# Reordering an eight-core decoder kernel: service order on ACT and DVE, one ones-matmul per norm, norms beside matmuls, gated first loads

## The chip, the cores and the metric

One Trainium2 chip, eight cores, the same program on each. The eight cores share the batch of 8 prompts and 32 samples: each takes one prompt of 2048 tokens (four tiles t0 to t3 of 512 tokens) and four samples of 8 tokens (one small tile TS of 32 tokens). The metric is the device time of the slowest core in microseconds (us), lower is better.

## The reference, cut to what matters

The function is one step of a two-layer decoder. Only its skeleton matters here: six RMS norms per tile, each of them in front of a large product.

```python
def rmsnorm(x, g):
    y = x * lax.rsqrt(jnp.mean(x * x, axis=-1, keepdims=True) + EPS)
    return y * g
# layer 0: x += 0.5*ffn(rms(x)); x += gla(rms(x));  x += 0.5*ffn(rms(x))
# shared:  k, v = proj(rms(x))                    (one norm statistic, two gains: this and the next FFN)
# layer 1: x += 0.5*ffn(rms(x)); x += attn(rms(x)); x += 0.5*ffn(rms(x))
def swiglu_ffn(x, w_in, w_out):           # 1024 -> 2*2688 -> 1024
    g, u = jnp.split(x @ w_in, 2, axis=-1)
    return (jax.nn.silu(g) * u) @ w_out
```

GLA is a gated linear attention, `attn` a dilated window attention over the shared keys and values.

## The kernel before

The kernel is a list scheduler that runs when the program is built. Every tile is a Python generator ("thread") that yields operations with their reads, writes and an estimated cost. The scheduler keeps a model time for each engine and each buffer and picks, again and again, among the operations that can start about earliest, the one of best rank to append next to its engine's list. Each engine is then given its list in exactly this order. So a choice made in the model is frozen into the order of instructions.

```python
class Sched:
    DMA_BW = 340e3                        # bytes per us, of the model
    # op(): tf = t0 + cost + (0.25 if eng == PE else 0.12)   <- when the model lets a dependent operation start

class Threads:
    TIE = 0.15
    def run(self):
        # ... cut: advance every thread to its next operation ...
        cands = [(S.start_of(...), th) for th in self.live if th[3] is not None]
        m = min(c[0] for c in cands) + self.TIE
        th = min((c for c in cands if c[0] <= m), key=lambda c: (rank of c, age of c))[1]
        # ... the operation of th is appended to its engine ...
```

Two of the four large tiles are in work at a time, each with its own ring of four weight units (`rings`, 8192 columns per partition each). The rank favours the first tile until it leads by 24 units, and favours the operations behind a matmul (`post`, `evac`) over the matmuls.

The norm computed the eight squares on ACT, summed them over partitions and over chunks by eight matmuls with a matrix of ones, and then applied the norm:

```python
    def norm_stats(T):
        # squares of 7 chunks must be in order before the first ones-matmul is
        yield mm(PS[b][:, 0:n], [(ones, T.h[:, m, :]) for m in range(7)], ...)
        yield mm(PS[b][:, 0:n], [(ones, T.h[:, 7, :])], ...)
        # Ln on ACT (with EPS), Exp(-0.5 x) on ACT
    def norm_apply(T, gcol, i):           # eight DVE operations h <- x * gain * rs
        for m in range(8): yield stt(T.h[:, m, :], T.x[:, m, :], ...)
```

Loads at the start: x of t0 and four weight units are issued first, x of t1 waits for weight unit 3, and the constants (`CF`) stand behind x in the issuing queue. In the trace of core 7 they are issued only at 25.8 us and land at 40.3 us.

The softmax here doesn't subtract the row's maximum and nothing guards it: scores larger than these inputs give would overflow.

Of the kernel before, what the change touches and what calls it, by code (L numbers as in the profile page):

```python
# [24 lines left out]
class Sched:  # L25



    DMA_BW = 340e3
    DMA_LAT = 2.2  # L30
# [16 lines left out]
    def _split(reads, writes):  # L47
# [4 lines left out]
        return reads, writes  # L52

    def start_of(self, eng, reads, writes):
        t = self.free[eng]
        reads, writes = self._split(reads, writes)
        for r in reads:
            k = self.lastw.get(r)
            if k is not None and k[3] > t:
                t = k[3]  # L60
        for w in writes:
            k = self.lastw.get(w)
            if k is not None and k[3] > t and not (k[2] == eng == PE):
                t = k[3]
            for k in self.readers.get(w, ()):
                if k[3] > t and not (k[2] == eng == PE):
                    t = k[3]
        return t
# [78 lines left out]
class Threads:  # L147
# [10 lines left out]
    def spawn(self, gen, rank, base=None):  # L158

        self.seq += 1  # L160
        self.live.append([rank, self.seq, gen, None, None, base or (lambda: 0)])

    def run(self):
        S = self.S
        while self.live:
# [34 lines left out]
            m = min(c[0] for c in cands) + self.TIE  # L200
            th = min((c for c in cands if c[0] <= m), key=lambda c: (c[1][0] + c[1][5](), c[1][1]))[1]
            _, eng, fn, reads, writes, cost, dma, nbytes = th[3]
# [16 lines left out]
def c_act(n):  # L219
    return 0.11 + n * 0.00083  # L220


def c_dve(n, rate=1):
    return 0.07 + n / (960.0 * rate)

# [72 lines left out]
def build():  # L298
# [116 lines left out]
    for t in range(4):  # L415
# [6 lines left out]
        def ffn_units(f):  # L422
            for j in range(NF):
                add_unit("fi%d" % f, j, wfi[f * NF + j], 2048)
            for m in range(8):
                add_unit("fo%d" % f, m, wfo[f * 8 + m], 2688)
        ffn_units(0)
        for gi, kind in enumerate(("v", "qk", "r", "o")):
            for i in range(4):
                add_unit(kind, i, wgl[gi * 4 + i], 2048)  # L430
            if t == 0 and kind == "qk":
                for s in range(4):
                    src = st_in[s * 4:(s + 1) * 4].rearrange("h p d -> p h d")
                    add_unit("S0", s, src, 2048, 1)
                    add_unit("S0b", s, src, 1024, 1)
        ffn_units(1)
# [16 lines left out]
    NWS = 8  # L453

    def weights(slot):
        ring = rings[slot]
        live = []
        off = 0
        if slot == 1:
            yield need(lambda: S.lastw.get(("x", "b1", 7)) is not None)  # L460
        for k, u in enumerate(order[slot]):
# [5 lines left out]
            yield need(lambda over=over: all(o.left == 0 for _, _, o in over))  # L467
            live = [x for x in live if x not in over] + [(lo, hi, u)]
            u.ap = ring[:, lo:hi]
            dst = u.ap  # L470
            if u.kind == "S0":
                dst = dst.bitcast(F32)
            if u.kind in ("S0", "S0b"):
                dst = dst.rearrange("p (h d) -> p h d", h=4)
            yield O(PL, (lambda e, u=u, dst=dst: e.dma_start(out=dst, in_=u.src)),  # L475
                    [("x", "b1", 1)] if u.uid == (1, "fi0", 0) else [], writes=[u.key] + [o.key for _, _, o in over], cost=1.0, dma="w%d_%d" % (slot, k % NWS), nbytes=u.n * 512)
            u.ready = True
# [126 lines left out]
    def load_x(T, prev):  # L604
        nq = 4 if T.n == 512 else 1
        if T.t == 1:
            yield need(lambda: units[(0, "fi0", 3)].ready)
        for q in range(nq):
            ms = range(q * 8 // nq, (q + 1) * 8 // nq)
            if prev is not None:  # L610
                yield need(lambda: all(("y", prev.nm, m) in done for m in ms))
            w = len(ms) * T.n
            src = xp[T.t] if T.n == 512 else xs
            yield O(SP, (lambda e, q=q, w=w, src=src, ms=ms: e.dma_start(
                out=T.x[:, ms[0]:ms[-1] + 1, :].rearrange("p m n -> p (m n)"), in_=src[:, q * w:(q + 1) * w])),
                [units[(0, "fi0", 3)].key] if T.t == 1 else [], writes=[xk(T, m) for m in ms], cost=0.1, dma="x%s_%d" % (T.b, q), nbytes=w * 512)
            for m in ms:
                yield square(T, m)
                done.add(("sq", T.nm, T.sqn, m))

    def square(T, m):
        return act(T.h[:, m, :], T.x[:, m, :], AF.Square, T.n, [xk(T, m)], [hk(T, m)], scale=1.0 / 32)

    def norm_stats(T):

        n = T.n
        sqn = T.sqn
        yield need(lambda: all(("sq", T.nm, sqn, m) in done for m in range(7)))
        (b,) = yield from get_banks(1)
        yield mm(PS[b][:, 0:n], [(ones, T.h[:, m, :]) for m in range(7)], [hk(T, m) for m in range(7)] + ["CB"], b, n, stop=False)  # L630
        yield need(lambda: ("sq", T.nm, sqn, 7) in done)
        yield mm(PS[b][:, 0:n], [(ones, T.h[:, 7, :])], [hk(T, 7), "CB"], b, n, start=False)
        (i,) = yield from T.pool.get("rs", 1, 1)
# [7 lines left out]

    def norm_apply(T, gcol, i):
        for m in range(8):
            yield stt(T.h[:, m, :], T.x[:, m, :], G[:, gcol + m:gcol + m + 1], T.pool.aps[i], ALU.mult, ALU.mult, T.n,
                      [xk(T, m), T.pool.key(i), "CF"], [hk(T, m)])

    def norm(T, gcol):
        i = yield from norm_stats(T)
        yield from norm_apply(T, gcol, i)
        T.pool.put("rs", i)  # L650

# [9 lines left out]
    def ffn(T, f, last):  # L661
# [14 lines left out]
        for j in range(NF):  # L676
# [8 lines left out]
            if j == 0 and n == 512:  # L685

                for kt in range(8):
                    for z, dst in ((0, g), (1, up)):
                        yield mm(dst, [(v[:, kt, z * 128:(z + 1) * 128], T.h[:, kt, :])], [hk(T, kt), u.key], bs[z], n, start=(kt == 0), stop=(kt == 7))
            else:  # L690
                yield mm(g, [(v[:, kt, 0:128], T.h[:, kt, :]) for kt in range(8)], hks(T) + [u.key], bs[0], n)
                yield mm(up, [(v[:, kt, 128:256], T.h[:, kt, :]) for kt in range(8)], hks(T) + [u.key], bs[-1], n)
# [21 lines left out]
    def tail(T, m, last):  # L714
# [7 lines left out]
        else:  # L722
            sqn = T.sqn
            yield square(T, m)
            done.add(("sq", T.nm, sqn, m))

# [6 lines left out]
    def gla(T):  # L733
# [4 lines left out]
        (b,) = yield from get_banks(1)  # L738
        yield mm(PS[b][0:16, :], [(WLR[:, kt, :], T.h[:, kt, :]) for kt in range(8)], h8 + ["WLR"], b, n)
        (gi,) = yield from pool.get("glr", 1, 1)  # L740
# [199 lines left out]
    def gla_s(T):  # L940
# [19 lines left out]
        (b,) = yield from get_banks(1)  # L960
        yield mm(PS[b][0:16, 0:n], [(WLR[:, kt, :], T.h[:, kt, :]) for kt in range(8)], h8 + ["WLR"], b, n)
        glr = R[0:16, 2432:2464]
# [62 lines left out]
        for s in range(4):  # L1025
            c8 = slice(s * 8, s * 8 + 8)
            us, ub = (yield from use(T, "S0", s)), (yield from use(T, "S0b", s))
            S0 = us.ap.bitcast(F32).rearrange("p (h w) -> p h w", h=4)
            S0b = ub.ap.rearrange("p (h w) -> p h w", h=4)
            (b,) = yield from get_banks(1)  # L1030
            po = PS[b][:, 0:64].rearrange("p (m n) -> p m n", m=8)
# [102 lines left out]
    def kv(T, tab):  # L1134
# [20 lines left out]
        u = yield from use(T, "kv", 0)  # L1155
        v = u.ap.rearrange("p (kt c) -> p kt c", kt=8)
        for kc in range(2):
            (b,) = yield from get_banks(1)
            yield mm(PS[b][:, 0:n], [(v[:, kt, kc * 128:(kc + 1) * 128], T.h[:, kt, :]) for kt in range(8)], h8 + [u.key], b, n)
            TH.spawn(kpost(kc, b), -4, T.rank)  # L1160
        u.left -= 1
# [45 lines left out]
    def qproj(T, tab):  # L1207
# [13 lines left out]
        for q in range(3):  # L1221
            u = yield from use(T, "wq", q)
            v = u.ap.rearrange("p (kt c) -> p kt c", kt=8)
            for z in range(2):
                (b,) = yield from get_banks(1)
                yield mm(PS[b][:, 0:n], [(v[:, kt, z * 128:(z + 1) * 128], T.h[:, kt, :]) for kt in range(8)], hks(T) + [u.key], b, n)
                TH.spawn(qpost(2 * q + z, b), -4, T.rank)
            u.left -= 1
# [245 lines left out]
    def tile_thread(T, prev):  # L1474
        T.sqn = 0
        yield from load_x(T, prev)
# [8 lines left out]
        i = yield from norm_stats(T)  # L1485
        yield from norm_apply(T, 48, i)
        yield from kv(T, tab)
        yield from norm_apply(T, 24, i)
        T.pool.put("rs", i)
        yield from ffn(T, 2, False)  # L1490
# [7 lines left out]


    S.op(PL, lambda e: e.dma_start(out=CB[:], in_=cbd[:, :]), [], ["CB"], cost=1.0, dma="c1", nbytes=B_END * 512)  # L1500
    TH.spawn(weights(0), -30)
    TH.spawn(weights(1), -29)

    def prologue():
        yield need(lambda: S.lastw.get(("x", "b0", 7)) is not None)
        yield O(SP, lambda e: e.dma_start(out=CF[:], in_=cfd[:, :]), [], ["CF"], cost=0.1, dma="c0", nbytes=A_END * 512)
        yield O(PL, lambda e: e.dma_start(out=WG2[:], in_=gg2[:, :]), [], ["WG2"], cost=1.0, dma="c2", nbytes=32768)
# [96 lines left out]
```

## Time and profile before

| | before |
|---|---|
| median time, 3 runs | 2539.63 us |
| span of the slowest core in the profile | 2532.5 us |
| PE (TensorE matmul) busy | 2375.8 us, 94% |
| ACT, DVE busy | 47%, 44% |
| granted TensorE clock, mean of 8 cores | 0.984 |

The page of the profile, its first part: busy time of each engine, share of the span, number of instructions.

```profile
span 2532.5 us, 42560 instructions; the slowest of 8 cores (2497.2 to 2532.5 us)
PE 2375.8 (94%) x14828; PEld 1146.6 (45%) x14828; DVE 1122.1 (44%) x2012; ACT 1198.3 (47%) x2312; POOL 319.9 (13%) x602
```

PE is the bound, with about 157 us of the span not busy. Where the idle time lies is told by the waits of PE (the same core): who it waited for, us in total, times, longest.

```profile
engine line waited for: us in total, times, longest us
PE pst L579 <- ACT h L584: 36.3, 11, 24.7
PE pst L579 <- DMA ring<-wfo: 25.9, 20, 5.1
PE pst L579 <- DVE r L592: 21.0, 5, 7.0
PE pst L579 <- DMA ring<-wfi: 15.8, 18, 2.0
PE pst L579 <- DMA CB<-cbd: 12.0, 1, 12.0
...
```

L579 is the helper through which nearly all matmuls go, so the name after the arrow carries the meaning. `h` from ACT are the squares: PE stood at the start until they could be summed. `wfo` and `wfi` are FFN weights. The windows view of the same core, 20 us each (columns: stretch, length, busy us and instructions of PE, PEld, DVE, ACT, POOL, then granted clock, DMA share, GB/s), over the last GLA stage:

```profile
1740.00:1760.00 20.00, 20.00 (x118) 10.15 (x117) 10.08 (x19) 8.63 (x16) 2.94 (x6) 1.00 0.95 159
1760.00:1780.00 20.00, 19.45 (x124) 9.97 (x122) 10.04 (x20) 17.48 (x34) 1.81 (x4) 1.00 0.62 110
1780.00:1800.00 20.00, 14.14 (x79) 6.52 (x77) 14.03 (x23) 18.97 (x34) 1.58 (x3) 0.95 0.77 154
1800.00:1820.00 20.00, 16.62 (x67) 7.04 (x68) 8.91 (x14) 5.32 (x9) 2.11 (x4) 0.80 0.38 62
```

ACT, 47% busy on average, is busy 8.63 us in the first of these stretches and 18.97 of 20 us in the third. There PE falls to 14.14, and the granted clock sinks to 0.80 in the stretch after.

The ones-matmuls stand in the groups of the page (count, then busy us and mean ns):

```profile
L579 PE MATMUL pst<-h,CB 128*128 128x512 bf16 x192 | 50.8, 397 | 37.1 <-ACT h L584 36.3
```

The start of PE, timeline view (start, us, engine, line, what, count, idle before):

```profile
37.04 3.15 PE L579 MATMUL pst<-h,CB 128*128 128x512 bf16 x7 [24.66 <-ACT h L584]
...
54.44 3.20 PE L579 MATMUL pst<-h,CB 128*128 128x512 bf16 x8 [9.93 <-ACT h L584]
57.48 10.52 PE L579 MATMUL pst<-h,ring 128*128 128x512 bf16 x48
```

The second of these lines is the norm of tile t1. It stands in PE's order before the first FFN of t0, which therefore starts at 57.48 us.

### The profile page before, as it was taken

The page shows a single profiled execution, that of the slowest core. Times are in us where ns is not written, and L with a number is a line of the kernel's source. Part 1 is how long each engine was busy: PE and PEld are TensorE (multiplying, and loading weights), DVE is VectorE, ACT ScalarE, POOL GpSimd, SP SyncE. Part 2 cuts the span into 40 slices and gives each one's busy share as a digit, 9 for nine tenths or more (in the row PEclk, how much of TensorE's full clock was granted, in tenths as well). Part 3 has the DMA queues.
Part 4 walks back from the last instruction along what each step waited for, and adds up shares of the span by engine and source line. Part 5 has one row for each costly group of instructions (what it writes and reads, how often), then busy time and mean ns, then how long its engine had stood idle before and what let it go on. Part 6 is the DMA issues. An engine that isn't in the chain of part 4 may idle for free.

```text
span 2532.5 us, 42560 instructions; the slowest of 8 cores (2497.2 to 2532.5 us)
## 1 busy us (share of the span) xinstructions
PE 2375.8 (94%) x14828; PEld 1146.6 (45%) x14828; DVE 1122.1 (44%) x2012; ACT 1198.3 (47%) x2312; POOL 319.9 (13%) x602
## 2 busy tenths in 40 slices
PE   2999999989999998999999899899899999999997
PEld 1445444544444444445444355345344444444443
DVE  1424563453632464446343144534544344634631
ACT  2634464563553365456353145545545335644541
POOL 1111111101111111111111011111011111011010
PEclk8999999999999998999999999999999999999999
DMA  7877787758878979976998978678689989598686
GB/s 147 136 128 123 150 140 124 134 85 145 154 138 135 171 123 171 169 118 126 166 166 146 191 130 139 117 134 145 123 141 182 152 149 178 91 150 146 126 142 129
DMA packets 103473, 358.29 MB, mean 141 GB/s; under 512 B 12592, under 2 KB 19424, under 8 KB 103136
## 3 DMA queue, kind: packets, MB, share of 16 engines
q0 software_dynamic: 86144, 327.05, 77.4%
q1 hardware_dynamic: 17120, 28.52, 3.7%
q8 instruction: 123, 2.02, 0.3%
q14 instruction: 86, 0.70, 0.1%
HBM read 665.04 MB, written 15.40 MB: 269 GB/s over the span
## 4 chain that ended last, share of the span: by engine, by line
PE 72%; DMA 15%; ACT 4%; DVE 4%; issue 3%; SPq 0%; POOL 0%; ACTq 0%; DVEq 0%; POOLq 0%
PE pst L579 69%; DMA ring<-wfi 6%; DMA ring<-wfo 6%; ACT p L584 2%; DVE h L595 2%; DMA x<-xp 1%; DMA ring<-wgl 1%; DMA kp<-p 1%; DVE p L592 1%; DMA ring<-cv 1%; ACT h L584 1%; DVE r L592 1%; DMA vp<-p 1%; PE pst L1332 0%; ACT Sbf L926 0%
## 5 line engine op out<-in xcount | busy, mean ns | idle before, releaser
L579 PE MATMUL pst<-h,ring 128*128 128x512 bf16 x6144 | 1388.0, 381 | 7.0 <-DMA ring<-wfi 2.8
L579 PEld LDWEIGHTS pst<-h,ring 128*128 128x128 bf16 x6144 | 591.0, 98 | 704.5 <-issue 35.5
L579 PE MATMUL pst<-r,ring 128*128 128x512 bf16 x3136 | 720.5, 385 | 37.7 <-DVE r L592 20.4
L584 ACT ACTIVATE p<-p 128x512 f32<-128x512 f32 x856 | 537.7, 630 | 83.5 <-DVE p L756 10.9
L592 DVE TENSOR_TENSOR p<-p,pst 128x512 f32<-128x512 f32 x368 | 252.0, 685 | 594.2 <-ACT p L584 587.7
L579 PEld LDWEIGHTS pst<-r,ring 128*128 128x128 bf16 x3136 | 304.7, 99 | 410.3 <-issue 67.9
L584 ACT ACTIVATE p<-pst 128x512 f32<-128x512 f32 (+1 forms) x472 | 279.2, 593 | 414.8 <-PE pst L579 398.0
L584 ACT ACTIVATE h<-x 128x512 bf16<-128x512 f32 x192 | 118.7, 627 | 472.7 <-DVE x L595 320.7
L475 POOL DMA_DIRECT2D ring<-wfi x336 | 177.5, 529 | 1194.8 <-PE pst L579 1080.1
L592 DVE TENSOR_TENSOR r<-p,pst 128x512 bf16<-128x512 f32 x336 | 230.6, 687 | 54.2 <-DVE p L592 45.7
L595 DVE SCALAR_TENSOR_TENSOR x<-pst,x 128x512 f32<-128x512 f32 x128 | 88.1, 689 | 270.6 <-PE pst L579 270.0
L595 DVE SCALAR_TENSOR_TENSOR h<-x,CF,p 128x512 bf16<-128x512 f32 x224 | 152.4, 746 | 64.5 <-PE pst L579 34.4
L475 POOL DMA_DIRECT2D ring<-wfo x128 | 67.6, 529 | 545.4 <-PE pst L579 462.1
L579 PE MATMUL pst<-h,CB 128*128 128x512 bf16 x192 | 50.8, 397 | 37.1 <-ACT h L584 36.3
L579 PE MATMUL pst<-ring,h 128*128 128x256 bf16 x640 | 74.4, 273 | 0.0
L579 PEld LDWEIGHTS pst<-hsb,ring 128*128 128x128 bf16 x1536 | 49.9, 96 | 45.1 <-issue 31.5
L592 DVE TENSOR_TENSOR x<-x,pst 128x512 f32<-128x512 f32 x64 | 43.8, 686 | 57.8 <-PE pst L579 57.8
L579 PE MATMUL pst<-hsb,ring 128*128 128x32 bf16 x1536 | 52.7, 176 | 17.0 <-DMA ring<-wfi 13.0
L475 POOL DMA_DIRECT2D ring<-wgl x64 | 33.8, 529 | 271.2 <-PE pst L579 245.2
L584 ACT ACTIVATE spb<-pst 128x32 f32<-128x32 f32 (+2 forms) x111 | 21.7, 196 | 95.9 <-PE pst L579 93.5
L579 PEld LDWEIGHTS pst<-ring,h 128*128 128x128 bf16 x640 | 61.4, 98 | 12.0 <-issue 2.7
L588 ACT COPY r<-pst 128x512 f32<-128x512 f32 (+3 forms) x104 | 50.6, 486 | 14.8 <-PE pst L1360 6.4
(145 smaller groups left out, 1072.6 us busy)
## 6 DMA issues: line engine op xcount, KB each, us to landing
ring<-wfi POOLq DMA_DIRECT2D x336, 512.0 KB, 7.1
ring<-wfo POOLq DMA_DIRECT2D x128, 672.0 KB, 8.1
ring<-wgl POOLq DMA_DIRECT2D x64, 512.0 KB, 6.3
x<-xp SPq DMA_DIRECT2D x16, 512.0 KB, 10.0
y_p<-x SPq DMA_DIRECT2D x32, 256.0 KB, 8.2
ring<-wqd POOLq DMA_DIRECT2D x12, 512.0 KB, 6.4
ring<-wod POOLq DMA_DIRECT2D x16, 384.0 KB, 7.5
ring<-wkv POOLq DMA_DIRECT2D x8, 512.0 KB, 5.9
```

The lines of the kernel that those rows point to most:

```text
L475: yield O(PL, (lambda e, u=u, dst=dst: e.dma_start(out=dst, in_=u.src)), [("x", "b1", 1)] if u.uid == (1, "fi0", 0) else [], writes=[u.key ...
L579: ins = e.matmul(out, lhsT=l, rhs=r, start=(start and i == 0), stop=(stop and i == last), skip_group_check=skip)
L584: return O(ACT, lambda e: e.activation(out=out, in_=in_, func=func, scale=scale, bias=bias), reads, writes, c_act(n))
L588: return O(ACT, lambda e: e.copy(out=out, in_=in_), reads, writes, c_act(n))
L592: return O(DVE, lambda e: e.tensor_tensor(out=out, in0=a, in1=b, op=op), reads, writes, c_dve(n, rate))
L595: return O(DVE, lambda e: e.scalar_tensor_tensor(out=out, in0=a, scalar=s, in1=b, op0=op0, op1=op1), reads, writes, c_dve(n))
```

## The change

Its intent: (1) ACT and DVE serve the operation that has waited longest, not the one of best rank; (2) the eight squares are summed by DVE, so that one ones-matmul is left per norm; (3) the norm's eight `h` operations are a thread of their own, and matmuls that follow take each chunk as it comes; (4) the first loads are gated by order; (5) every other of the last FFN output weights goes to the ring of the other tile slot, idle by then. Besides: the model's costs of ACT and DVE follow the trace, and its DMA bandwidth goes from 340 to 330. A small one: a bf16 copy of the sample states comes from ACT instead of a second load.

```diff
     def start_of(self, eng, reads, writes):
-        t = self.free[eng]
+        t = self.free[eng] if eng else 0.0
+    def ready(self, reads, writes):
+        return self.start_of(None, reads, writes)
+    def urgency(self, th):
+        eng, rank = th[3][1], th[0] + th[5]()
+        if eng in (ACT, DVE):
+            return (self.S.ready(th[3][3], th[3][4]) + self.FAVOUR * rank, th[1])   # FAVOUR = 0.02
+        return (-1e9 + rank, th[1])
-            th = min((c for c in cands if c[0] <= m), key=lambda c: (c[1][0] + c[1][5](), c[1][1]))[1]
+            th = min((c for c in cands if c[0] <= m), key=lambda c: self.urgency(c[1]))[1]
 ...
     def square(T, m):
-        return act(T.h[:, m, :], T.x[:, m, :], AF.Square, ...)
+        yield act(T.h[:, m, :], T.x[:, m, :], AF.Square, ...)
+        # 512-token tiles: acc (f32) <- acc + square on DVE, the eighth sum goes to h (bf16)
 ...
-        yield mm(PS[b][:, 0:n], [(ones, T.h[:, m, :]) for m in range(7)], ...)
-        yield mm(PS[b][:, 0:n], [(ones, T.h[:, 7, :])], ..., start=False)
+        ms = [T.sum] if n == 512 else range(8)
+        yield mm(PS[b][:, 0:n], [(ones, T.h[:, m, :]) for m in ms], ...)
 ...
     def norm_apply(T, gcol, i, free=True):
+        def apply(): ...                       # the eight operations, each marks its chunk as done
+        TH.spawn(apply(), -2, T.rank)
 ...
+                if (t, f) == (3, 3) and m % 2 == 0:
+                    order[0].append(order[1].pop())
 ...
+    first = {(0, "fi0", 1): [("x", "b0", 5)]}                     # unit 1 after six chunks of x of t0
+    for k in range(4):
+        first[(1, "fi0", k)] = [units[(0, "fi0", 12 + 2 * k)].key]  # second ring: after units 12, 14, 16, 18 of the first
+                after = units[(0, "fi0", 3 + 2 * q)]              # x of t1, quarter q: after units 3, 5, 7, 9
```

More of the change, by code (lines that the diff above doesn't have):

```diff
@@ L25 @@
 class Sched:
-    DMA_BW = 340e3
+    DMA_BW = 330e3
     DMA_LAT = 2.2
@@ L161, in spawn @@
         self.live.append([rank, self.seq, gen, None, None, base or (lambda: 0)])
+    def urgency(self, th):
[3 more added lines that the diff above has]
+        return (-1e9 + rank, th[1])
+    FAVOUR = 0.02
     def run(self):
@@ L219, in c_act @@
 def c_act(n):
-    return 0.11 + n * 0.00083
+    return 0.19 + n * 0.00084
 def c_dve(n, rate=1):
-    return 0.07 + n / (960.0 * rate)
+    return 0.16 + n / (960.0 * rate)
 def c_mm(count, n):
@@ L434, in build @@
                     add_unit("S0", s, src, 2048, 1)
-                    add_unit("S0b", s, src, 1024, 1)
+                    add_unit("S0b", s, None, 1024, 1)
         ffn_units(1)
@@ L458, in weights @@
         off = 0
-        if slot == 1:
-            yield need(lambda: S.lastw.get(("x", "b1", 7)) is not None)
+        yield need(lambda: S.lastw.get(("x", "b0", 7)) is not None)
         for k, u in enumerate(order[slot]):
@@ L467, in weights @@
             yield need(lambda over=over: all(o.left == 0 for _, _, o in over))
-            live = [x for x in live if x not in over] + [(lo, hi, u)]
+            live = [x for x in live if x not in over] + [(lo, hi, u)] + [(a, lo, o) for a, b, o in over if a < lo] \
+                + [(hi, b, o) for a, b, o in over if b > hi]
             u.ap = ring[:, lo:hi]
+            if u.uid in first:
+                yield need(lambda: all(k in S.lastw for k in first[u.uid]))
             dst = u.ap
             if u.kind == "S0":
-                dst = dst.bitcast(F32)
-            if u.kind in ("S0", "S0b"):
-                dst = dst.rearrange("p (h d) -> p h d", h=4)
+                dst = dst.bitcast(F32).rearrange("p (h d) -> p h d", h=4)
+            if u.src is None:
+                u.keys = [u.key] + [o.key for _, _, o in over]
+                u.ready = True
+                continue
             yield O(PL, (lambda e, u=u, dst=dst: e.dma_start(out=dst, in_=u.src)),
-                    [("x", "b1", 1)] if u.uid == (1, "fi0", 0) else [], writes=[u.key] + [o.key for _, _, o in over], cost=1.0, dma="w%d_%d" % (slot, k % NWS), nbytes=u.n * 512)
+                    first.get(u.uid, []), writes=[u.key] + [o.key for _, _, o in over], cost=1.0, dma="w%d_%d" % (slot, k % NWS), nbytes=u.n * 512)
             u.ready = True
@@ L605, in load_x @@
         nq = 4 if T.n == 512 else 1
-        if T.t == 1:
-            yield need(lambda: units[(0, "fi0", 3)].ready)
         for q in range(nq):
@@ L611, in load_x @@
                 yield need(lambda: all(("y", prev.nm, m) in done for m in ms))
+            if T.t == 1:
+                after = units[(0, "fi0", 3 + 2 * q)]
+                yield need(lambda: after.ready)
             w = len(ms) * T.n
@@ L615, in load_x @@
                 out=T.x[:, ms[0]:ms[-1] + 1, :].rearrange("p m n -> p (m n)"), in_=src[:, q * w:(q + 1) * w])),
-                [units[(0, "fi0", 3)].key] if T.t == 1 else [], writes=[xk(T, m) for m in ms], cost=0.1, dma="x%s_%d" % (T.b, q), nbytes=w * 512)
-            for m in ms:
-                yield square(T, m)
-                done.add(("sq", T.nm, T.sqn, m))
+                [after.key] if T.t == 1 else [], writes=[xk(T, m) for m in ms], cost=0.1, dma="x%s_%d" % (T.b, q), nbytes=w * 512)
+        for m in range(8):
+            yield from square(T, m)
     def square(T, m):
-        return act(T.h[:, m, :], T.x[:, m, :], AF.Square, T.n, [xk(T, m)], [hk(T, m)], scale=1.0 / 32)
+        sqn = T.sqn
+        yield act(T.h[:, m, :], T.x[:, m, :], AF.Square, T.n, [xk(T, m)], [hk(T, m)], scale=1.0 / 32)
+        if T.n == 512:
+            k = T.nsq
+            T.nsq = (k + 1) % 8
+            yield need(lambda: T.nadd == k)
+            if k == 0:
+                (T.acc,) = yield from T.pool.get("acc", 1, 1)
+                T.sum = m
+            else:
+                acc, ka = T.pool.aps[T.acc], T.pool.key(T.acc)
+                a, ra = (T.h[:, T.sum, :], hk(T, T.sum)) if k == 1 else (acc, ka)
+                o, wa = (T.h[:, m, :], hk(T, m)) if k == 7 else (acc, ka)
+                yield tt(o, a, T.h[:, m, :], ALU.add, 512, [ra, hk(T, m)], [wa])
+                T.sum = m
+            T.nadd = (k + 1) % 8
+            if k == 7:
+                T.pool.put("acc", T.acc)
+        done.add(("sq", T.nm, sqn, m))
     def norm_stats(T):
@@ L627, in norm_stats @@
         sqn = T.sqn
-        yield need(lambda: all(("sq", T.nm, sqn, m) in done for m in range(7)))
+        yield need(lambda: all(("sq", T.nm, sqn, m) in done for m in range(8)))
         (b,) = yield from get_banks(1)
-        yield mm(PS[b][:, 0:n], [(ones, T.h[:, m, :]) for m in range(7)], [hk(T, m) for m in range(7)] + ["CB"], b, n, stop=False)
-        yield need(lambda: ("sq", T.nm, sqn, 7) in done)
-        yield mm(PS[b][:, 0:n], [(ones, T.h[:, 7, :])], [hk(T, 7), "CB"], b, n, start=False)
+        ms = [T.sum] if n == 512 else range(8)
+        yield mm(PS[b][:, 0:n], [(ones, T.h[:, m, :]) for m in ms], [hk(T, m) for m in ms] + ["CB"], b, n)
         (i,) = yield from T.pool.get("rs", 1, 1)
@@ L640, in norm_stats, with norm_apply, apply, mmh @@
         return i
-    def norm_apply(T, gcol, i):
-        for m in range(8):
-            yield stt(T.h[:, m, :], T.x[:, m, :], G[:, gcol + m:gcol + m + 1], T.pool.aps[i], ALU.mult, ALU.mult, T.n,
-                      [xk(T, m), T.pool.key(i), "CF"], [hk(T, m)])
+    def norm_apply(T, gcol, i, free=True):
+        T.hn += 1
+        hn = T.hn
+        def apply():
+            for m in range(8):
+                yield stt(T.h[:, m, :], T.x[:, m, :], G[:, gcol + m:gcol + m + 1], T.pool.aps[i], ALU.mult, ALU.mult, T.n,
+                          [xk(T, m), T.pool.key(i), "CF"], [hk(T, m)])
+                done.add(("h", T.nm, hn, m))
+            if free:
+                T.pool.put("rs", i)
+        TH.spawn(apply(), -2, T.rank)
     def norm(T, gcol):
         i = yield from norm_stats(T)
-        yield from norm_apply(T, gcol, i)
-        T.pool.put("rs", i)
+        norm_apply(T, gcol, i)
+    def mmh(T, outs, lhs, reads, bs, n):
+        hn = T.hn
+        for kt in range(8):
+            yield need(lambda: ("h", T.nm, hn, kt) in done)
+            for z in range(len(outs)):
+                yield mm(outs[z], [(lhs(kt, z), T.h[:, kt, :])], [hk(T, kt)] + reads, bs[z], n, start=(kt == 0), stop=(kt == 7))
     def hks(T):
@@ L685, in ffn @@
             if j == 0 and n == 512:
-                for kt in range(8):
-                    for z, dst in ((0, g), (1, up)):
-                        yield mm(dst, [(v[:, kt, z * 128:(z + 1) * 128], T.h[:, kt, :])], [hk(T, kt), u.key], bs[z], n, start=(kt == 0), stop=(kt == 7))
-            else:
+                yield from mmh(T, (g, up), lambda kt, z: v[:, kt, z * 128:(z + 1) * 128], [u.key], bs, n)
+            else:
+                hn = T.hn
+                yield need(lambda: ("h", T.nm, hn, 7) in done)
                 yield mm(g, [(v[:, kt, 0:128], T.h[:, kt, :]) for kt in range(8)], hks(T) + [u.key], bs[0], n)
@@ L722, in tail @@
         else:
-            sqn = T.sqn
-            yield square(T, m)
-            done.add(("sq", T.nm, sqn, m))
+            yield from square(T, m)
     def resid(T, m, b, src, n):
@@ L738, in gla @@
         (b,) = yield from get_banks(1)
-        yield mm(PS[b][0:16, :], [(WLR[:, kt, :], T.h[:, kt, :]) for kt in range(8)], h8 + ["WLR"], b, n)
+        yield from mmh(T, (PS[b][0:16, :],), lambda kt, z: WLR[:, kt, :], ["WLR"], (b,), n)
         (gi,) = yield from pool.get("glr", 1, 1)
@@ L960, in gla_s @@
         (b,) = yield from get_banks(1)
-        yield mm(PS[b][0:16, 0:n], [(WLR[:, kt, :], T.h[:, kt, :]) for kt in range(8)], h8 + ["WLR"], b, n)
+        yield from mmh(T, (PS[b][0:16, 0:n],), lambda kt, z: WLR[:, kt, :], ["WLR"], (b,), n)
         glr = R[0:16, 2432:2464]
@@ L1029, in gla_s @@
             S0b = ub.ap.rearrange("p (h w) -> p h w", h=4)
+            yield copy(ACT, S0b, S0, 1024, [us.key], ub.keys)
             (b,) = yield from get_banks(1)
@@ L1156, in kv @@
         v = u.ap.rearrange("p (kt c) -> p kt c", kt=8)
+        bs = yield from get_banks(2)
+        yield from mmh(T, [PS[b][:, 0:n] for b in bs], lambda kt, z: v[:, kt, z * 128:(z + 1) * 128], [u.key], bs, n)
         for kc in range(2):
-            (b,) = yield from get_banks(1)
-            yield mm(PS[b][:, 0:n], [(v[:, kt, kc * 128:(kc + 1) * 128], T.h[:, kt, :]) for kt in range(8)], h8 + [u.key], b, n)
-            TH.spawn(kpost(kc, b), -4, T.rank)
+            TH.spawn(kpost(kc, bs[kc]), -4, T.rank)
         u.left -= 1
@@ L1223, in qproj @@
             v = u.ap.rearrange("p (kt c) -> p kt c", kt=8)
+            bs = yield from get_banks(2)
+            yield from mmh(T, [PS[b][:, 0:n] for b in bs], lambda kt, z: v[:, kt, z * 128:(z + 1) * 128], [u.key], bs, n)
             for z in range(2):
-                (b,) = yield from get_banks(1)
-                yield mm(PS[b][:, 0:n], [(v[:, kt, z * 128:(z + 1) * 128], T.h[:, kt, :]) for kt in range(8)], hks(T) + [u.key], b, n)
-                TH.spawn(qpost(2 * q + z, b), -4, T.rank)
+                TH.spawn(qpost(2 * q + z, bs[z]), -4, T.rank)
             u.left -= 1
@@ L1474, in tile_thread @@
     def tile_thread(T, prev):
-        T.sqn = 0
+        T.sqn = T.hn = T.nsq = T.nadd = 0
         yield from load_x(T, prev)
@@ L1485, in tile_thread @@
         i = yield from norm_stats(T)
-        yield from norm_apply(T, 48, i)
+        norm_apply(T, 48, i, False)
         yield from kv(T, tab)
-        yield from norm_apply(T, 24, i)
-        T.pool.put("rs", i)
+        norm_apply(T, 24, i)
         yield from ffn(T, 2, False)
@@ L1497, in tile_thread @@
         yield from ffn(T, 3, True)
+    S.op(SP, lambda e: e.dma_start(out=CF[:], in_=cfd[:, :]), [], ["CF"], cost=0.1, dma="c0", nbytes=A_END * 512)
     S.op(PL, lambda e: e.dma_start(out=CB[:], in_=cbd[:, :]), [], ["CB"], cost=1.0, dma="c1", nbytes=B_END * 512)
@@ L1504, in prologue @@
     def prologue():
-        yield need(lambda: S.lastw.get(("x", "b0", 7)) is not None)
-        yield O(SP, lambda e: e.dma_start(out=CF[:], in_=cfd[:, :]), [], ["CF"], cost=0.1, dma="c0", nbytes=A_END * 512)
         yield O(PL, lambda e: e.dma_start(out=WG2[:], in_=gg2[:, :]), [], ["WG2"], cost=1.0, dma="c2", nbytes=32768)
```

## The prediction

> **What bounds it.** TensorE. The page gives PE 2375.8 of 2532.5 us busy (94%), against ACT 47%, DVE 44%, and 0.75 to 0.93 DMA share in the stages (windows view). Back-to-back 128x512 matmuls start every 0.2166 us (224 in 48.51 us, timeline)[...]. [...]what counts is its instructions plus about 157 us of idle time. By the PE waits: 49 us before 57.5 us (CB 12.0, "ACT h" 34.6: squares waiting for x; tile 1's stand in PE's order ahead of tile 0's FFN), about 15 us in the last 63 us, mostly waits for wfo and the last output, and some 90 us scattered: wfo and wfi loads 35, "DVE r" 21 in five waits of up to 7 us (end of the GLA), the rest small.
>
> **What changes, costed.**
> 1. Ones-matmuls of six norms in each of four 512-token tiles go from 192 to 24. 168 x 0.2166 = 36 us less PE streaming. I expect 30 realised: the DMA share is already 0.93 from 1200 to 1400 us. Added: 168 DVE adds of about 0.69 us (the 128x512 f32 tensor_tensor), 116 us, taking DVE from 44% to about 50%; off the critical path, except about 0.9 us in each norm chain, which the other tile should cover.
> 2. Start: only tile 0's x, the constants and one weight unit compete at first, not 10 MB; CF is no longer behind blocked x loads (it now lands at 40 us). About 3.5 MB at the 200 GB/s of the first 20 us is an estimated 17 us, plus square, add, ones-matmul, Ln, Exp, first h (about 4.5 us): tile 0's first FFN matmul at about 24 us instead of 57.5. Part goes back, as x of tile 1 and the second ring then load beside a FFN that consumes a unit in about 4 us: net 27 us.
> 3. Tail: half the last wfo units use the idle other ring: waits of 7.4 us (2400 us to the end) shrink by 6.
> 4. Longest-waiting-first and chunk-wise norms, with costs that match the trace (ACT 0.63, DVE 0.69): PSUM banks come back more evenly, but critical GLA chains lose priority. Net gain perhaps 10 us of the scattered waits; the clock after long stalls (0.80 to 0.86 in 20 us slices near 580, 1610, 1810 us) improves a little.
>
> Sum: 30 + 27 + 6 + 10 = 73 us: **2466 us, range 2428 to 2502**. Chances: faster by over 2% 0.80, within 2% 0.18, slower 0.02.
>
> **What would show each step.** Page, groups: `pst<-h,CB` ones-matmuls x24, PE busy about 2340; new DVE adds x168, about 115 us, DVE about 50%. Timeline: first `h,ring` 128x512 matmul between 20 and 30 us; PE busy in the first 63 us about 40 us instead of 14. PE waits: "ACT h" down from 36 to about 8, wfo from 26 to under 20; "DVE r" and "ACT p" roughly as before or lower. Last 63 us: no wfo wait over 1 us. Granted clock 0.98 to 0.99.
>
> **What would make it wrong.** The start stays DMA-bound ([...]wfi waits from 25 to 110 us give back 15 us or more). First-come service delays the chains that release PE, so "DVE r" and "ACT p" waits double. Loads, now with less slack, take the saved PE time: wfo and wfi waits rise by 20 us or more. In the other direction, smoother bank release removes most of the scattered idle time: about 2420 us.

The sum came to 30 + 27 + 6 + 10 = 73 us, taken from the 2539.63 us of before, and the 36 us of the first term are 168 times the 0.2166 us between matmuls in before's trace (core 7, 224 matmuls in 48.51 us from 2431.63 us on).

## The result, and the profile after

| | before | after |
|---|---|---|
| median (all runs) | 2540.32 us | 2456.03 us |
| fast runs | 2535.99, 2539.63, 2541.0 | 2452.8, 2455.28, 2456.78 |
| left out, slow | 2615.4 | 2547.06 |

The ratio is 0.9674, with a 95% interval of 0.9653 to 0.9694. Ratios here and below are the mean time of one kernel's fast runs over the mean of the other's fast runs of the same rounds, so not quite the ratio of the medians quoted. Executions in which one die ran at a lower clock are left out of the means. The change is faster by 3.3%, 83 us.

The page after, and the waits of PE on its slowest core (core 0). The helper is now L604, ACT's L609, DVE's L617 and L620.

```profile
span 2451.3 us, 42368 instructions; the slowest of 8 cores (2404.4 to 2451.3 us)
PE 2308.7 (94%) x14405; PEld 1129.3 (46%) x14660; DVE 1217.6 (50%) x2180; ACT 1173.8 (48%) x2316; POOL 317.1 (13%) x598
```

```profile
engine line waited for: us in total, times, longest us
PE pst L604 <- DMA ring<-wfi: 43.8, 29, 3.6
PE pst L604 <- DMA ring<-wfo: 30.3, 26, 3.5
PE pst L604 <- DMA CB<-cbd: 11.0, 1, 11.0
PE pst L604 <- DVE hsb L620: 6.8, 1, 6.8
...
PE pst L604 <- DVE r L617: 3.5, 3, 2.1
...
PE pst L604 <- ACT h L609: 0.9, 3, 0.6
```

One trap: this core shows 14405 matmuls against 14660 weight loads, so about 255 matmul records are missing and its PE busy time is too low. Cores whose records are complete have 2316 to 2327 us. The waits for squares are gone (36.3 to 0.9), `DVE r` fell from 21.0 to 3.5, and the waits for weights rose.

The groups by form on core 2, a core with complete records (the last three columns as before): 24 ones-matmuls are left, and 120 + 24 + 24 = 168 DVE additions have come, 0.69 us each.

```profile
L604 PE MATMUL pst<-h,CB 128*128 128x512 bf16 x24 | 9.3, 387 | 5.6 <-DVE spb L617 5.4 <-DVE h L617 0.2
...
L617 DVE TENSOR_TENSOR p<-p,h 128x512 f32<-128x512 f32 x120 | 82.6, 689 | 49.9 <-ACT h L609 47.3 <-DVE p L617 1.4 <-ACT KTs L613 0.7
...
L617 DVE TENSOR_TENSOR h<-p,h 128x512 bf16<-128x512 f32 x24 | 16.6, 691 | 13.5 <-ACT h L609 13.0 <-DVE p L617 0.5
L617 DVE TENSOR_TENSOR p<-h 128x512 f32<-128x512 bf16 x24 | 16.5, 689 | 16.5 <-ACT h L609 8.2 <-ACT spb L609 8.2
```

The start of PE after, timeline view, core 0:

```profile
23.33 0.58 PE L604 MATMUL pst<-h,CB 128*128 128x512 bf16 x1 [4.48 <-DVE spb L617]
27.47 0.59 PE L604 MATMUL pst<-hsb,ring 128*128 128x32 bf16 x16 [3.56 <-DMA ring<-wfi]
27.89 3.57 PE L604 MATMUL pst<-h,ring 128*128 128x512 bf16 x8
```

The FFN of t0 starts at 27.89 us instead of 57.48. The 3.56 us before it are a wait for weight unit 1: the small tile's use of that unit stands in PE's order ahead of t0's use of unit 0.

**The sums over all cores.** Single cores differ, so I added up each core's PE waits by the engine waited for and took the mean of the eight cores. The experiments are in the same table (mean core; us). "PE busy" suffers a little from missing records in all kernels.

| kernel | ratio to before | mean span | waits DMA | waits ACT | waits DVE | PE busy |
|---|---|---|---|---|---|---|
| before | 1 | 2515.4 | 51.4 | 47.7 | 37.9 | 2364.7 |
| after | 0.9674 | 2429.4 | 70.5 | 4.7 | 24.1 | 2318.2 |
| after, eight ones-matmuls (a_ones8) | 0.9754 | 2450.1 | 59.1 | 12.4 | 13.8 | 2352.7 |
| after, rank order (a_rank) | 0.9826 | 2469.6 | 73.9 | 10.2 | 44.7 | 2326.0 |
| after, old start (a_start) | 0.9739 | 2447.5 | 63.2 | 3.6 | 51.8 | 2317.3 |
| after, old tail (a_tail) | 0.9702 | 2443.0 | 81.2 | 6.3 | 23.6 | 2320.6 |
| after, rank order, tie 0.10 (a_rank_tie10) | 0.9625 | 2423.7 | 69.3 | 4.5 | 24.3 | 2314.0 |
| before, tie 0.10 (b_tie10) | 0.9814 | 2471.1 | 54.1 | 41.5 | 11.1 | 2351.0 |
| before, longest wait first (b_fifo) | 0.9834 | 2470.4 | 47.8 | 40.8 | 14.7 | 2351.2 |
| before, tie 0.115 (b_tie115) | 0.9812 | 2479.6 | 60.5 | 41.6 | 10.6 | 2353.4 |
| before, tie 0.14 (b_tie14) | 1.0001 | 2521.4 | 53.8 | 48.3 | 37.6 | 2367.9 |
| after, bandwidth 340 (a_bw340) | 0.9662 | 2427.7 | 73.8 | 2.0 | 21.9 | 2318.1 |
| after, norms inline (a_inline) | 0.9651 | 2423.0 | 67.5 | 5.1 | 23.6 | 2315.2 |
| after, tie 0.10, bandwidth 345 (a_tie10_bw345) | 0.9686 | 2439.3 | 82.5 | 2.5 | 20.6 | 2322.1 |

From before to after the mean core lost 86 us: 38 of PE's waits (43 of ACT and 14 of DVE less, 19 of DMA more) and about 46 of PE's busy time, where the 168 matmuls taken away are worth 36 by the prediction's estimate. The rest, 10 us, fits the clock: the mean granted clock rose from 0.984 to 0.990, and 0.6% of 2364.7 us is 14 us (an estimate, which takes PE's busy time to go with the clock, as in the 11 and 22 matmuls counted under "The clock" below).

The table has one profile of each kernel, and its columns have noise of their own. The last three rows do the changed kernel's work in another order, and their waits for DMA lie between 67.5 and 82.5 us. So a difference of some 10 us in this column is a hint and no proof.

### The profile page after: what moved, and what is told of

Read it like the earlier page. It is cut to its first block, busy times and chain, and to the rows that moved or that the text cites. A ratio compares the mean times of both kernels' runs of the same rounds, so it can differ in the third digit from the quotient of the medians.

```text
span 2451.3 us, 42368 instructions; the slowest of 8 cores (2404.4 to 2451.3 us)
## 1 busy us (share of the span) xinstructions
PE 2308.7 (94%) x14405; PEld 1129.3 (46%) x14660; DVE 1217.6 (50%) x2180; ACT 1173.8 (48%) x2316; POOL 317.1 (13%) x598
## 4 chain that ended last, share of the span: by engine, by line
PE 71%; DMA 25%; issue 3%; ACT 1%; DVE 1%; POOLq 0%; SPq 0%; POOL 0%; ACTq 0%; DVEq 0%
PE pst L604 68%; DMA ring<-wfi 13%; DMA ring<-wfo 9%; DMA ring<-wod 1%; DMA x<-xp 1%; DMA ring<-wgl 1%; PE pst L1389 0%; ACT p L609 0%; PE pst L1328 0%; DMA ring<-wkv 0%; PE pst L959 0%; PE pst L1350 0%; ACT h L609 0%; ACT r L613 0%; PE pst L976 0%
## 5 line engine op out<-in xcount | busy, mean ns | idle before, releaser
L604 PE MATMUL pst<-h,ring 128*128 128x512 bf16 x5980 | 1371.0, 381 | 31.1 <-DMA ring<-wfi 15.7
L604 PEld LDWEIGHTS pst<-h,ring 128*128 128x128 bf16 x6144 | 590.6, 98 | 719.3 <-issue 52.7
L604 PE MATMUL pst<-r,ring 128*128 128x512 bf16 x3056 | 704.4, 383 | 26.0 <-DMA ring<-wfo 18.5
L609 ACT ACTIVATE p<-p 128x512 f32<-128x512 f32 x856 | 534.6, 629 | 71.9 <-DVE p L812 11.7
L609 ACT ACTIVATE p<-pst 128x512 f32<-128x512 f32 (+1 forms) x472 | 279.2, 596 | 494.2 <-PE pst L604 478.0
L617 DVE TENSOR_TENSOR p<-p,pst 128x512 f32<-128x512 f32 x368 | 252.0, 686 | 507.6 <-ACT p L609 506.7
L604 PEld LDWEIGHTS pst<-r,ring 128*128 128x128 bf16 x3136 | 303.5, 98 | 385.4 <-issue 39.6
L609 ACT ACTIVATE h<-x 128x512 bf16<-128x512 f32 x192 | 118.7, 627 | 371.9 <-DVE x L620 268.6
L617 DVE TENSOR_TENSOR r<-p,pst 128x512 bf16<-128x512 f32 x336 | 230.3, 686 | 42.5 <-DVE p L617 36.1
L620 DVE SCALAR_TENSOR_TENSOR x<-pst,x 128x512 f32<-128x512 f32 x128 | 88.2, 689 | 212.4 <-PE pst L604 204.2
L620 DVE SCALAR_TENSOR_TENSOR h<-x,CF,p 128x512 bf16<-128x512 f32 x224 | 150.9, 745 | 14.8 <-ACT p L609 14.4
L617 DVE TENSOR_TENSOR p<-p,h 128x512 f32<-128x512 f32 x120 | 82.6, 689 | 49.5 <-ACT h L609 47.2
L604 PE MATMUL pst<-hsb,ring 128*128 128x32 bf16 x1536 | 53.1, 177 | 37.0 <-DMA ring<-wfi 28.0
L604 PEld LDWEIGHTS pst<-hsb,ring 128*128 128x128 bf16 x1536 | 50.3, 96 | 64.9 <-issue 52.0
L609 ACT ACTIVATE spb<-pst 128x32 f32<-128x32 f32 (+2 forms) x111 | 21.7, 198 | 109.2 <-PE pst L604 107.2
L604 PE MATMUL pst<-ring,h 128*128 128x256 bf16 x640 | 73.9, 273 | 0.0
L604 PEld LDWEIGHTS pst<-ring,h 128*128 128x128 bf16 x640 | 61.5, 98 | 11.8 <-issue 2.7
L617 DVE TENSOR_TENSOR x<-x,pst 128x512 f32<-128x512 f32 x64 | 43.9, 686 | 30.4 <-PE pst L604 29.2
```

Of the source, the lines that this page charges most:

```text
L604: ins = e.matmul(out, lhsT=l, rhs=r, start=(start and i == 0), stop=(stop and i == last), skip_group_check=skip)
L609: return O(ACT, lambda e: e.activation(out=out, in_=in_, func=func, scale=scale, bias=bias), reads, writes, c_act(n))
L617: return O(DVE, lambda e: e.tensor_tensor(out=out, in0=a, in1=b, op=op), reads, writes, c_dve(n, rate))
L620: return O(DVE, lambda e: e.scalar_tensor_tensor(out=out, in0=a, scalar=s, in1=b, op0=op0, op1=op1), reads, writes, c_dve(n))
```

## The experiments

Twelve kernels ran, in three batches, all correct. 0.001 of ratio is 2.5 us. The ratio of "after" comes from its own batch, and a difference between two kernels of different batches is uncertain by some 6 to 8 us, as their intervals show. The new costs of ACT and DVE, the bf16 copy and the matmuls by chunk were not undone singly.

Three theories stood at first. W, the one of the prediction: the gain is PE work taken away plus the earlier start. L: the loads took much of it back. S: the service order of ACT and DVE is the main gain.

### a_ones8: only the sum on DVE undone

```diff
-        if T.n == 512:            # sum the squares on DVE
+        if False:
-        ms = [T.sum] if n == 512 else range(8)
+        ms = range(8)
```

> The changed kernel with only the squares' sum undone: eight ones-matmuls per norm again, no DVE adds. Theory W (work and start: most of the 84 us is PE work taken away plus the earlier start): 25 to 36 us slower than the changed kernel (2481 to 2492 us, ratio to before about 0.978), PE busy up by about 36 us, DVE busy down by about 115 us. Theory L (loads took the saved PE time back: the waits for weights rose by 19 us on the mean core): under 15 us slower (below 2471), with the PE's waits for DMA 20 us or more below the changed kernel's.

Measured: 2474.78 us median, ratio 0.9754 (0.9740 to 0.9768), so 20 us slower than the changed kernel: between the two expectations. PE busy rose by 34.5 us on the mean core, as expected. But the waits for DMA were 11 us lower, as L says, if not 20. So the sum on DVE takes some 35 us of work from PE, and some 14 of them are not gained. Of these the profile shows 11 as waits for DMA, which is within the spread of that column, so L is likely here but not shown; the waits for ACT and DVE together moved by under 3 us (8 less, 10 more).

### a_rank: only the service order undone

```diff
-        if eng in (ACT, DVE):
+        if False:
             return (self.S.ready(...) + self.FAVOUR * rank, th[1])
```

> The changed kernel with only the longest-waiting-first rule for ACT and DVE undone (rank alone decides, as before). Theory W: within 10 us of the changed kernel (2446 to 2466), as ACT and DVE are half idle. Theory S (the service order is the main gain): 20 us or more slower (above 2476), and the PE's waits for DVE results at the end of the GLA stage, up to 7 us each and 21 us in sum before, come back.

Measured: 2493.95 us, ratio 0.9826 (0.9812 to 0.9840): 39 us slower than the changed kernel. Theory S is right, and W, which had allowed 10 us, is wrong on this term: this is the largest single part of the change. On the mean core the waits for DVE rose from 24 to 45 us. On core 7 of this kernel the GLA's long waits are back (PE waits, three of its lines):

```profile
PE pst L604 <- DMA ring<-wfi: 38.5, 26, 5.2
PE pst L604 <- DMA ring<-wfo: 16.7, 18, 3.9
PE pst L604 <- DVE r L617: 16.5, 3, 9.4
...
```

### a_start: only the order of the first loads undone

```diff
-    first = {(0, "fi0", 1): [("x", "b0", 5)]} ...   # and the gates on x of t1 and on the second ring
+    first = {(1, "fi0", 0): [("x", "b1", 1)]}       # x of t1 after unit 3, constants behind x, as before
```

> The changed kernel with only the gating and order of the first loads undone (constants behind x, four weight units at once, x of the second tile after unit 3). Theory W: 20 to 28 us slower (2476 to 2484), first 128x512 FFN matmul after 50 us, PE busy in the first 63 us 15 us instead of 36, PE waits for squares about 35 us again. Theory L: the head start is given back in later waits for weights, so under 10 us slower.

Measured: 2470.23 us, ratio 0.9739 (0.9725 to 0.9753): 16 us slower. The first FFN matmul stood at 57.6 us again. PE's busy time in the first 63 us is 11.8 us on the mean core, against 36.4 in the changed kernel, so the head start is 25 us. The waits moved from ACT to DVE (51.8), so the name I had expected was wrong: on core 7 the longest, 28.5 us, is for the small tile's norm, which DVE reaches at 39.1 us, behind additions of squares and the constants. Of the 25 us, 9 are not gained; 7 may have come back as waits for DMA (63.2 without the head start, 70.5 with it), again within the spread of that column.

### a_bw340: a mere reshuffle

```diff
-    DMA_BW = 330e3
+    DMA_BW = 340e3
```

> The changed kernel with the schedule model's DMA bandwidth set back from 330 to 340: it reorders over a thousand lines of the instruction lists but adds and takes away no work. Every theory: within 8 us of the changed kernel (2448 to 2464). How far it moves is how much a mere reshuffle of the order is worth, and the yardstick for the other runs.

Measured: 2447.48 us, ratio 0.9662 (0.9642 to 0.9682), 3 us from the changed kernel, inside the noise. One reordering without an aim moved the time little, which makes it unlikely that the 39 us of the service order are an accident of order; two sharper tests of that follow.

### What in the service order? a_rank_tie10 and b_tie10

Reading the scheduler again showed a rival cause. A dependent operation of ACT or DVE may start 0.12 us after its producer in the model, and candidates within TIE = 0.15 us of the earliest start compete by rank. So when an engine comes free, the next step of the chain it has just served is a candidate although it is not ready yet, and if its rank is better it passes over work that has been ready all along. With a window under 0.12 us it is no candidate. Theory T: this is what the new rule repairs. Theory F: it is first-come service itself that counts.

```diff
-    TIE = 0.15
+    TIE = 0.1
```

That one line was put into the kernel before (b_tie10), and into the changed kernel with the rule undone (a_rank_tie10).

> The changed kernel with the longest-waiting-first rule undone (rank decides, as in the run that was about 38 us slower than the changed kernel) and the scheduler's tie window cut from 0.15 to 0.10 us. The model lets a dependent operation start 0.12 us after its producer, so with 0.15 a chain's next step competes with work that has been ready all along, and with 0.10 it does not. Theory T (the rule's gain is that ready work is no longer passed over for a chain's next step of better rank): within 12 us of the changed kernel (ratio to before 0.963 to 0.972), DVE and ACT waits of the PE near 29 us on the mean core instead of 55. Theory F (what counts is first-come service itself, the order among waiting operations): still 25 us or more slower than the changed kernel (ratio above 0.977).

> The kernel before with nothing changed but the tie window, 0.15 to 0.10 us: the same instructions in another order. Theory T: 15 to 30 us faster than before (ratio 0.988 to 0.994). Theory F: within 8 us (0.997 to 1.003).

Measured: a_rank_tie10 2436.98 us, ratio 0.9625 (0.9599 to 0.9652), 51 us faster than a_rank and at least as fast as the changed kernel. b_tie10 2487.35 us, ratio 0.9814 (0.9790 to 0.9838): 47 us from one constant, more than the 15 to 30 that I had put down. On the mean core b_tie10 has 27 us less of waits for DVE and 6 less for ACT than before, 14 us less PE busy time, and 0.9875 of clock instead of 0.9839. The last GLA stage of b_tie10, in the windows view of core 7, comes about 25 us earlier than before:

```profile
1700.00:1720.00 20.00, 20.00 (x105) 9.41 (x103) 9.62 (x17) 9.11 (x15) 3.16 (x6) 1.00 0.84 135
1720.00:1740.00 20.00, 20.00 (x122) 10.29 (x121) 10.23 (x20) 14.02 (x26) 2.11 (x4) 1.00 0.69 116
1740.00:1760.00 20.00, 19.40 (x121) 9.96 (x120) 11.90 (x22) 17.22 (x33) 1.58 (x3) 1.00 0.85 143
1760.00:1780.00 20.00, 20.00 (x103) 9.27 (x101) 12.47 (x21) 13.63 (x25) 2.63 (x5) 1.00 0.91 170
```

ACT has the same kind of peak (17.22 of 20 us), but it is spread over three stretches (14.0, 17.2, 13.6) where before it was 17.5 and 19.0 after 8.6. PE stays full and its clock at 1.00. The waits of PE of this core no longer show a GLA term among the large ones:

```profile
PE pst L579 <- ACT h L584: 37.0, 3, 26.0
PE pst L579 <- DMA ring<-wfo: 28.4, 20, 4.7
PE pst L579 <- DMA ring<-wfi: 17.7, 18, 2.1
PE pst L579 <- DMA CB<-cbd: 11.8, 1, 11.8
...
PE pst L579 <- DVE r L592: 1.6, 2, 1.4
```

### b_fifo: the rule alone on the kernel before

The diff of `start_of`, `urgency` and `run` above, nothing else.

> The kernel before with only the longest-waiting-first rule for ACT and DVE added. If the rule works by itself: 20 to 38 us faster (ratio 0.985 to 0.992), PE waits for DVE below 25 us. If it pays only together with the squares' sum, which loads the DVE by another 116 us: within 10 us (0.996 to 1.004).

Measured: 2494.0 us, ratio 0.9834 (0.9797 to 0.9871), 42 us faster. The rule works by itself, without the sum on DVE, and does what the small window does (the intervals overlap, and the waits by engine are nearly the same).

### b_tie115 and b_tie14: is it the 0.12?

If 0.10 were just a lucky order, its neighbours would fall anywhere. So the window was set just under and just over the hand-over time.

```diff
-    TIE = 0.15
+    TIE = 0.115        # b_tie115;  0.14 in b_tie14
```

> The kernel before with the tie window at 0.115 us, just under the 0.12 us at which the scheduler's model lets a dependent operation of ACT or DVE start after its producer. Theory T (the threshold is that hand-over time): as fast as with 0.10, ratio to before 0.978 to 0.985. Theory R (0.10 was a lucky reshuffle, and any other order falls somewhere between): ratio anywhere, most likely 0.988 to 1.002.

> The kernel before with the tie window at 0.14 us, just over the 0.12 us hand-over. Theory T: like before, ratio 0.994 to 1.004, with the PE waits for DVE near 38 us on the mean core. Theory R: as likely fast as slow.

Measured: b_tie115 2492.74 us, ratio 0.9812 (0.9785 to 0.9838); b_tie14 2540.44 us, ratio 1.0001 (0.9977 to 1.0026). The step lies between 0.115 and 0.14, where theory T puts it. b_tie14 has before's waits (37.6 us for DVE on the mean core), b_tie115 has b_tie10's (10.6). No run lies in between, at 0.125 for example, and the model has other times in this interval (before's cost of an ACT operation on 32 columns is 0.137 us). So the place of the step agrees with the 0.12 us but does not single it out. The waits of PE on core 6 of b_tie14, to be held against those of b_tie10 above:

```profile
PE pst L579 <- ACT h L584: 37.8, 12, 25.0
PE pst L579 <- DMA ring<-wfo: 30.9, 21, 3.7
PE pst L579 <- DVE r L592: 21.0, 5, 7.2
...
```

### a_inline: norms in the tile's own thread again

```diff
-        TH.spawn(apply(), -2, T.rank)
+        yield from apply()
```

> The changed kernel with the norm's eight chunk operations run in the tile's own thread again, so that only after the last of them may the following matmuls be put in order; otherwise the same work. If running norms beside matmuls matters: 8 us or more slower, with PE waits for h of 10 us more. If not, as I expect, since the other tile has matmuls to fill with: within 8 us of the changed kernel (ratio 0.964 to 0.971).

Measured: 2443.86 us, ratio 0.9651 (0.9626 to 0.9675), not slower than the changed kernel. The thread of its own for norms is worth nothing that these runs can show. The matmuls by chunk (`mmh`) stayed in this kernel, so what they alone do was not tried.

### a_tail: the last output weights in one ring again

```diff
-                if (t, f) == (3, 3) and m % 2 == 0:
+                if False:
```

> The changed kernel with only the move of every other last output weight to the idle ring undone. As predicted blind: 4 to 8 us slower (ratio to before 0.9690 to 0.9706 where the changed kernel has 0.9674), with waits for wfo of about 7 us in the last 70 us. If the loads were only shifted: within 2 us.

Measured: 2462.03 us, ratio 0.9702 (0.9678 to 0.9725): 7 us slower, as predicted, though the intervals overlap. The trace shows it where it should be. From 2390 us to the end the changed kernel has no wait for `wfo` at all on core 0; here the slowest core has this:

```profile
PE pst L604 <- DMA ring<-wfo: 6.7, 3, 3.3
```

### a_tie10_bw345: a version meant to beat both

```diff
-    TIE = 0.15
+    TIE = 0.1
-    DMA_BW = 330e3
+    DMA_BW = 345e3
```

> A version meant to beat both: the changed kernel with the tie window at 0.10 us and the model's DMA bandwidth at 345. If the tie window still matters beside the longest-waiting-first rule: 10 to 25 us faster than the changed kernel (ratio to before 0.957 to 0.964). If the rule had already removed what the window cost: within 8 us of it (0.964 to 0.971).

Measured: 2458.46 us, ratio 0.9686 (0.9663 to 0.9709): no better than the changed kernel. So the small window adds nothing visible to the rule, as it would if both cured one fault. But this kernel moved the bandwidth too, and its waits for DMA are the highest of all (82.5): that a gain of the window is hidden behind them was not tested. The best kernel is a_rank_tie10 (rank order, window 0.10), 0.9625 against 0.9674; the two come from different batches and their intervals just meet (0.9652, 0.9653), so whether it really is faster than the changed kernel is open.

## Why the prediction was right or wrong, point by point

The total was right: 2466 us predicted, 2456 measured, within the range and clearly faster. The sum hid three terms that were off, two one way and one the other.

| term | predicted | undone alone, on the chip |
|---|---|---|
| ones-matmuls | 30 us | 20 us (a_ones8) |
| start | 27 us | 16 us (a_start) |
| tail | 6 us | 7 us (a_tail) |
| service order, with chunk-wise norms and costs | 10 us | 39 us for the order (a_rank), about -6 for the norm's thread (a_inline, within noise) |
| sum | 73 us | 82 us without the last, of 83 measured |

That the single parts add up so well is partly luck; each carries some 6 to 8 us of uncertainty.

- **What bounds the kernel** was right: PE at 94% before and after.
- **The ones-matmuls**: the mechanism and its size on PE were right (24 left, 168 additions of 0.69 us, DVE at 50%, 34.5 us of PE work). The allowance for loads was too small. I took 6 us off; 14 were missing, 11 of them seen as waits for DMA.
- **The start**: the FFN came at 27.9 us (24 predicted, 20 to 30 allowed); "PE busy in the first 63 us about 40 us" was 36 on the mean core. The "200 GB/s of the first 20 us" was read too high: before's core 7 moved 161 GB/s in that time (201 from 5 to 15 us). The give-back was named but then the term was still sized too high.
- **"wfo from 26 to under 20" was wrong**: 30.3 on the slowest core, and `wfi` went from 15.8 to 43.8. The prediction had this as a danger ("Loads, now with less slack, take the saved PE time"), and it is probably where part of two gains went (14 of 34.5 us, 9 of 25 us).
- **The step that failed is the fourth**: "PSUM banks come back more evenly, but critical GLA chains lose priority. Net gain perhaps 10 us". The order was worth 39 us, and the GLA chains were the ones that gained. I had read ACT as half idle from its average of 47% and so had taken its order for unimportant. In the stage that stalled, ACT was busy 18.97 of 20 us, a number that my own windows view of before would have given. For the question asked here, whether ACT's order matters, the occupancy of the whole span (47%) misled, and that of the stage did not.
- **The clock**: predicted to "improve a little"; it rose from 0.984 to 0.990 on the mean core. With the order undone (a_rank) it is 0.984 again. In before, windows of 1 us on core 7 show 0.50 from 1798 to 1808 us, where PE waited from 1797.65 to 1803.38 us (the 5.7 us stall), and this makes the 0.80 of the slice. From 1803.5 to 1807.9 us, at 0.50, 11 matmuls with ring weights are counted; from 1812 to 1816.4 us, at 1.00, 22. What made the clock fall is not shown: it fell 0.3 us into that stall (0.96 in the window from 1797 to 1798), after a wait of 2.8 us just before it.

What is shown: that a tie window of at most 0.115 us instead of at least 0.14 is worth some 45 us, that the rule alone is worth about as much, and that the difference appears as PE's waits for DVE results, mostly in the GLA stage, and as clock. What is argued, not shown: that the 0.12 us hand-over is the reason and that rule and window cure the same fault; and which passed-over operation starts the chain of delays. Runs of just two chained 128x512 ACT operations on `p` are about as frequent in the fast order (328 in b_tie10) as in the slow one (354 in before), so a simple count of chains served to the end does not tell it; that stays open.

## What to carry to other kernels

In a list scheduler, compare the width of the tie window with the hand-over time that the model gives dependent operations: if it is wider, a rank can pull in work that is not ready ahead of work that is; here windows of 0.14 and 0.15 us beside a hand-over of 0.12 cost some 45 us against 0.10 and 0.115. Judge an engine's importance by its busy share in the stage where the bound engine waits, not by its average. And when work is taken from the bound engine while the DMA share is high (0.93 from 1200 to 1400 us before), allow for part of the gain to be lost: here 14 of 34.5 us and 9 of 25 us were, probably to waits for loads.

## What the runs show of the granted clock and of the hand-over

- In the fast runs here, before's and the changed kernel's among them with PE busy 94% of the slowest core's span, the eight cores were granted 0.977 to 0.994 on the mean of their spans. Only slow runs fall below that, mostly on one die: to 0.808 to 0.811 in a_rank's, to 0.941 to 0.944 in the changed kernel's.
- In the trace of before (core 7) DVE waited 0.18 us on average for `r` operations on its own `p` (48.5 us in 274 waits, the longest 0.5); the scheduler's 0.12 us was under it. One such pair came at 0.11 us (a `p` that ended at 1783.45 us, an `r` that started at 1783.56).
